# Weights' parts and lower rows at other byte offsets in a decoder layer's products

## The chip, the cores and the metric

The kernel runs on one core of a Trainium2 chip. It computes one inference step of a decoder layer in a single launch. The metric is the device time of that launch in microseconds; the time before is the median of 3 runs. A traced execution of the same kernel gives the profile, in microseconds unless marked ns.

## The reference

There are 288 tokens: 256 of a prompt and 8 groups of 4 sample tokens. The model's width is 2048. What is computed, cut to its core:

```python
h = rms_norm(x, norm1)
z = h @ w_in            # queries, keys, values, gates: 12 816 columns
q, k, v, (...) = split(z)
o_swa = sliding_window_attention(q, k, v, sink)
o_g = gated_linear_attention(...)         # per-head norm, swish gate
y = sigmoid(gs) * (o_swa @ p_swa) + sigmoid(gg) * (o_g @ p_gla)
x = x + y @ w_o
h2 = rms_norm(x, norm2)
x = x + square(relu(h2 @ w_up)) @ w_down  # 2048 -> 8192 -> 2048
y_out = rms_norm(x, final_norm)
```

The attention caches and the recurrent states are outputs too. All is float32.

## The kernel before

**Layout.** Activations stand with features on the 128 partitions and the 288 tokens along the free dimension: a tensor of 2048 features is 16 rows of 288 values on each partition. A matrix product has a 128x128 piece of the weights as the stationary operand and a row of 288 values as the moving one.

**Three products for one.** Each operand is split into an upper part (the value rounded to the format `fp32r`) and a lower part (what is left, in `fp32r` as well). Each piece of a product is then three products on TensorE: upper row by upper weight, lower row by upper weight, upper row by lower weight. The upper and lower rows are called `hh` and `hl` in the input projection, `o` (eight rows of upper and eight of lower parts in one tile) for `ps`, `gh` and `gl` for `pg`, `yh` and `yl` for `wo`, `h2h` and `h2l` for `up`, `uh` and `ul` for `dn`.

**The loop.** `gemm` (L222) makes 512 output columns of one product. It loads the weights in chunks of 256 rows by 512 columns (`raw`, six buffers, issued on SP's queue at L233). For each half of a chunk `wsplit` (L215) has ScalarE write the upper part `whi` (L218) and VectorE the lower part `wlo` (L156), five buffers each. A chunk is 24 products on TensorE (L251): two rows k by four slices m of 128 columns by the three of the split. In the first and the last chunk of a group the two rows alternate after every three products; in between all of one row come first. Four PSUM banks collect the results, and `evac` moves them out.

**Stages.** The order is the list `ORDER`: the input projection with the two attentions interleaved in small steps (`pump`), with `ps` in the middle; then `rg`, `pg` (four groups), `wo` (four groups), and four blocks b of `up{b}` (four groups) and `dn{b}` (four groups). A group has 8 chunks, in `ps` 4.

**Addresses.** Rows made by `rows` (L180) are 320 values apart, 1280 bytes, of which 288 are used, and start at multiples of 256 bytes; so do the buffers of `whi` and `wlo` (2048 bytes each). The rows of `o` are 288 values apart, 1152 bytes: every second one starts 128 bytes behind a multiple of 256. The weights `qx` of the attention's scores (L454) use two neighbouring buffers of 1152 bytes (tags `rs_m` and `rs_t`), the first at a multiple of 256, the second 128 bytes behind one.

**Other names in this text.** `ones` and `onesr` are the same 128x128 ones in float32 and `fp32r`. `maskp` is the mask of the prompt's scores, `masks` that of the samples' scores; the latter stands in the tile `ya`, in rows not yet needed. `at` is the gated attention's 128x384 matrix of products within a block: ScalarE copies it out of PSUM (L756, L757), GpSimd zeroes what lies ahead in time (L759), and TensorE uses it as the moving operand of `po` (L780, L781). `en` is a tile of that attention whose two buffers are read by the products that make `at`. `rso` is the tag of the two factors `rstd2` and `rstd3` of the last norms.

Of the kernel before, what the change touches and what calls it, by code (L numbers as in the profile page):

```python
# [12 lines left out]
F32 = mybir.dt.float32  # L13
F32R = mybir.dt.float32r
AF = mybir.ActivationFunctionType
ALU = mybir.AluOpType
# [3 lines left out]
P = 128  # L20
# [6 lines left out]
NT = TP + TS  # L27
# [31 lines left out]
def swa_rows():  # L59

    rows = []
    for p in range(2):
        for r in range(4):
# [8 lines left out]
         + ["qk2", "v2", "gg0", "gg1", "qk3", "v3", "gg2", "gg3"] + [f"rg{i}" for i in range(4)]  # L72
         + [f"pg{i}" for i in range(4)] + [f"wo{i}" for i in range(4)]
         + [x for b in range(4) for x in ([f"up{b}_{i}" for i in range(4)] + [f"dn{b}_{i}" for i in range(4)])])


def chunks_of(name):
    return 4 if name.startswith("ps") else 8
# [53 lines left out]
def step_kernel(ctx: ExitStack, tc: tile.TileContext, a: dict):  # L132
    nc = tc.nc
    V, S, G, T, SY = nc.vector, nc.scalar, nc.gpsimd, nc.tensor, nc.sync
    main = ctx.enter_context(tc.tile_pool(name="main", bufs=1))
# [4 lines left out]
    def f(ap):  # L140
        return ap.bitcast(F32)

    def bank(name):
        return psm.tile([P, 512], F32, name=name, tag="sm")

    def flat(ap):
        return ap.rearrange("p a b -> p (a b)")
# [7 lines left out]
    def sub(out, x, y, eng=V):  # L155
        eng.tensor_tensor(out, x, y, ALU.subtract)  # L156
# [1 line left out]

    ident = main.tile([P, P], F32, name="ident")
    norms = main.tile([P, 36], F32, name="norms")  # L160
    ones = main.tile([P, P], F32, name="ones")
    onesr = main.tile([P, P], F32R, name="onesr")
    epst = main.tile([P, 1], F32, name="epst")
    bm = main.tile([P, 32 + NB + 34], F32, name="bm")
# [4 lines left out]
    raw0 = main.tile([P, 1024], F32, name="raw", tag="raw", bufs=RAW)  # L169
    for s in range(2):  # L170
        S.dma_start(raw0[:, 512 * s:512 * s + 512], a["w"][0, :, 512 * s:512 * s + 512])
    V.memset(ones, 1.0)
    V.tensor_copy(onesr, ones)
    V.memset(epst, EPS)
    n2, fn, gn = norms[:, 0:16], norms[:, 16:32], norms[:, 32:36]

    def big(tag, name, dt=F32, n=KT):
        return main.tile([P, n, NT], dt, name=name, tag=tag)

    def rows(tag, name, n=KT):  # L180

        return main.tile([P, n, 320], F32R, name=name, tag=tag)[:, :, 0:NT]

    def exp_table():
        tc.keep_in_program_order(S.preload_act_table_set("natural_log_exp_and_others"))
# [16 lines left out]
    def pump(rates):  # L202
        for i, r in enumerate(rates):
            credit[i] += r
            while credit[i] >= 1.0:
                credit[i] -= 1.0
                if not step(queues[i]):
                    credit[i] = 0.0
# [3 lines left out]
            pass  # L212


    def wsplit(raw):  # L215
        hi = main.tile([P, 512], F32R, name="whi", tag="whi", bufs=5)
        lo = main.tile([P, 512], F32R, name="wlo", tag="wlo", bufs=5)
        S.copy(hi, raw)  # L218
        sub(lo, raw, f(hi))
        return hi, lo  # L220

    def gemm(name, xh, xl, evac, rate=(), first=None):  # L222
        nk = 2 * chunks_of(name)
        ps = [pmm.tile([P, 512], F32, name="mm", tag="mm") for _ in range(4)]
        for c in range(nk // 2):
            if FIRST[name] + c == 0:
                raw = raw0
            else:
                raw = main.tile([P, 1024], F32, name="raw", tag="raw", bufs=RAW)
                if first is not None:  # L230
                    first[0](c, raw)
                else:
                    SY.dma_start(raw, a["w"][FIRST[name] + c])  # L233
            parts = []
            for s in range(2):
                if first is not None:
                    first[1](2 * c + s)
                parts.append((2 * c + s, *wsplit(raw[:, 512 * s:512 * s + 512])))
            if first is not None:
                first[2](c)  # L240

            turns = c == nk // 2 - 1 or c == 0 and first is None
            order = [(i, m) for m in range(4) for i in range(2)] if turns else [(i, m) for i in range(2) for m in range(4)]
            order = [(i, m, j) for i, m in order for j in range(3)]
            if c == 0 and first is not None:

                order[:12] = [(0, m, j) for j in range(3) for m in range(4)]
            for i, m, j in order:
                k, hi, lo = parts[i]
                o, sl = ps[m][:, :NT], slice(m * P, m * P + P)  # L250
                T.matmul(o, lhsT=(lo if j == 2 else hi)[:, sl], rhs=xl(k) if j == 1 else xh(k),  # L251
                         start=k == 0 and j == 0, stop=k == nk - 1 and j == 2)
                if k == nk - 1 and j == 2:
                    evac(m, o)
            pump(rate)
# [39 lines left out]

    xa = big("SG", "x")
    hh, hl = rows("XH", "hh"), rows("XL", "hl")
    xn = []

# [97 lines left out]
    def swa(pool):  # L397
        rope = pool.tile([P, 2, NT], F32, name="rope")
        SY.dma_start(flat(rope), a["rope"])
        vt = pool.tile([P, 2, 2, P], F32, name="vt")  # L400
# [1 line left out]
        sinkb = pool.tile([P, 16], F32, name="sinkb")  # L402
        nsinkb = pool.tile([P, 16], F32, name="nsinkb")
        sinkr = pool.tile([P, 1], F32, name="sinkr")
        maskp = pool.tile([P, 384], F32, name="maskp")
        masks = ya[:, 8:12]
        SY.dma_start(sinkb, a["sinkb"])
        SY.dma_start(sinkr, a["sinkr"])
# [151 lines left out]
        po = bank("os")  # L560
        pov = po.rearrange("p (a b c) -> p a b c", a=4, b=2)
        sn = pool.tile([TS, 4, P], F32, name="stn", tag="sc", bufs=2)
        for pr in range(4):
# [8 lines left out]
            for p in range(2):  # L572
                for b in range(2):
                    T.matmul(pov[:, pr, p], lhsT=vc[p][:, 2 * pr + b], rhs=st[:, P * b + 64 * p:P * b + 64 * p + 64],  # L574
                             start=pr == 0 and p == 0 and b == 0, stop=False, skip_group_check=True)
# [32 lines left out]
    with tc.tile_pool(name="swa", bufs=1) as spool:  # L608
        RS = (1.05,)

        ya = big("YA", "ya")
# [7 lines left out]
    gpool = ctx.enter_context(tc.tile_pool(name="gla", bufs=1))  # L619
# [19 lines left out]
    def gla(h):  # L639
# [24 lines left out]
        vt = gpool.tile([P, 2, 512], F32, name="vtok", tag="vtok")  # L664
# [9 lines left out]
        for t in range(2):  # L674
            e = main.tile([P, 9, P], F32, name="e", tag=f"Za{2 + t}")
            en = gpool.tile([P, 2, P], F32, name="en", tag="en", bufs=2)
# [42 lines left out]
        pa = bank("pa")  # L719
# [32 lines left out]
            for work in tiled.pop():  # L752
                work()
        yield
        at = gpool.tile([P, 384], F32, name="at")
        S.copy(at, pa[:, :384])  # L756
        S.copy(at[0:64, 320:384], pa[64:P, 384:448])  # L757
        for sl, n in ((slice(0, 256), 256), (slice(256, 384), P)):
            G.affine_select(out=at[:, sl], in_=at[:, sl], pattern=[[1, n]], compare_op=ALU.is_ge, fill=0.0, base=0,  # L759
                            channel_multiplier=-1)  # L760
        yield
        parts = h < 3
        kdt = gpool.tile([P, 2, 256], F32R if parts else F32, name="kdt", tag="B")
# [12 lines left out]
        for jj in range(2):  # L776
            po = bank("po")
            for j in range(2):
                vsl = slice(P * (2 * jj + j), P * (2 * jj + j) + P)
                T.matmul(po[:, 256 * j:256 * j + 256], lhsT=vt[:, 0, vsl], rhs=at[:, 0:256], start=True, stop=False)  # L780
                T.matmul(po[:, 256 * j + P:256 * j + 256], lhsT=vt[:, 1, vsl], rhs=at[:, 256:384], start=False, stop=True)  # L781
            S.copy(o_g[:, 2 * jj:2 * jj + 2, 0:TP], po.rearrange("p (a b) -> p a b", a=2))
            if parts:
                S.copy(vh[:, jj], vt[:, jj])
                for c in (slice(0, 256), slice(256, 512)):
                    lo = main.tile([P, 256], F32R, name="vl", tag=("zr", "sr")[jj], bufs=2)
                    sub(lo, vt[:, jj, c], f(vh[:, jj, c]))
                    vl.append(lo)
            yield
# [120 lines left out]
    def start_head(h):  # L910
        queues[0].append(gla(h))
        queues[1].append(gla_sample(h))
# [5 lines left out]
    for j in range(4):  # L918
        sl = slice(4 * j, 4 * j + 4)
# [21 lines left out]
    for j in range(4):  # L941
        sl = slice(4 * j, 4 * j + 4)
# [3 lines left out]
    gh, gl = {}, {}  # L946
    for h in range(4):
        gh[h] = rows(f"Za{(0, 2, 3, 1)[h]}", f"gh{h}", 4)
        tt = main.tile([P, 4, NT], F32, name="tt", tag="tt")

        def rg_evac(m, ps):
            zr = main.tile([P, NT], F32, name="zr", tag="zr", bufs=2)
            sr = main.tile([P, NT], F32, name="sr", tag="sr", bufs=2)
            mul(zr, ps, rstd1)
            S.activation(sr, zr, AF.Sigmoid)
            mul(zr, zr, sr)
            mul(tt[:, m], og[h][:, m], zr)
            S.copy(gh[h][:, m], tt[:, m])
        if h == 2:
            late.append(True)  # L960
        gemm(f"rg{h}", H, L, rg_evac, rate=R3)
        if h == 1:
            drain(0)
        if h == 2:
            drain(1)
        gl[h] = rows(f"Zb{h}", f"gl{h}", 4)
        sub(gl[h], tt, f(gh[h]))
# [3 lines left out]
    yh, yl = rows("XH", "yh"), rows("XL", "yl")  # L971
# [15 lines left out]
    h2h = [rows(f"Za{j}", f"h2h{j}", 4) for j in range(4)]  # L987
    h2l = [rows(f"Zb{j}", f"h2l{j}", 4) for j in range(4)]
    acc2 = main.tile([P, NT], F32, name="acc2", tag="acc")
    rstd2 = main.tile([P, NT], F32, name="rstd2", tag="rso", bufs=2)  # L990

    def square_sum(acc, x, start):
        if start:
# [59 lines left out]


    acc3 = main.tile([P, NT], F32, name="acc3", tag="acc")
    rstd3 = main.tile([P, NT], F32, name="rstd3", tag="rso", bufs=2)
    last = []
    parts3 = []

# [70 lines left out]
    for n in (1, 1, 2, 2, 2, 2, 2, 2, 1, 1):  # L1130
        sl = slice(i, i + n)
# [57 lines left out]
def build(arrays):  # L1189
    nc = bacc.Bacc("TRN2", target_bir_lowering=False, num_devices=1)  # L1190
    aps = {}
    for n, v in arrays.items():
        aps[n] = nc.dram_tensor(f"in_{n}", v.shape, mybir.dt.from_np(v.dtype), kind="ExternalInput").ap()
    for n, s in OUTS.items():
        aps[n] = nc.dram_tensor(f"out_{n}", s, F32, kind="ExternalOutput").ap()
    with tile.TileContext(nc) as tc:
        step_kernel(tc, aps)
    return nc
# [21 lines left out]
```

## Time and profile before

| | us |
|---|---|
| time, median of 3 runs | 1754.13 |
| lowest and highest run | 1753.87, 1754.18 |
| the profiled execution | 1756.34 |
| its span | 1754.6 |
| TensorE busy in it | 1743.0 |
| VectorE busy | 1209.0 |
| ScalarE busy | 878.3 |

A profiled execution's span runs from its first to its last instruction. The lines by group give source line, engine, operation, output and inputs by tile name, shapes and count, then busy time, mean of one in ns, and the engine's idle time before them with what ended it. The weight load of a product has a row of its own (PEld) and overlaps the product before. Products overlap too: one lasts 0.29 us from its first to its last value, while the next starts much sooner, so the rate is read from starts or from counts in a window, not from the length of one. The DMA engines moved 214 GB/s on average; the weights come in ahead of their use:

```profile
raw<-in_w SPq DMA_DIRECT2D x518, 512.0 KB, 4.0
HBM read 348.58 MB, written 23.92 MB: 212 GB/s over the span
```

### The profile page before, as it was taken

Reading aid. Unit: us, or ns where it says so; the run is one execution under the profiler, and the core shown is the slowest. Engines: PE = TensorE matmul, PEld = TensorE weight load, DVE = VectorE, ACT = ScalarE, POOL = GpSimd, SP = SyncE. Lnnn points to the kernel's source line nnn. Section 1 sums busy time; section 2 is a strip of 40 time slices with the busy share of each in tenths; the row PEclk is TensorE's granted clock in tenths of the full one; section 3 lists DMA queues with packets and bytes.
Section 4 is the critical chain, followed back from the end, with each engine's and each line's share of the span. In section 5 each row is a group of like instructions: output and inputs, shape, how many; then the busy total and the mean of one; then the engine's idle time right before and its main releaser. Section 6 shows DMA issues by size and latency. Waiting matters only on the chain.

```text
span 1754.6 us, 34457 instructions
## 1 busy us (share of the span) xinstructions
PE 1743.0 (99%) x13463; PEld 1714.7 (98%) x13463; DVE 1209.0 (69%) x2270; ACT 878.3 (50%) x1650; POOL 63.4 (4%) x75
## 2 busy tenths in 40 slices
PE   9999999999999999999999999999999999999997
PEld 8999999999999999999999999999999999999997
DVE  8896574665836657666688677767777777777545
ACT  7555464444534645544445554455544554455543
POOL 0000001001001010000131000000000000000000
PEclk9999999999999999999999999999999999999998
DMA  8645446455464455444866777776777667765552
GB/s 296 213 140 181 135 162 228 158 192 207 158 234 167 159 217 180 165 165 154 326 213 210 263 253 260 276 263 240 249 256 286 237 233 287 269 247 201 191 176 95
DMA packets 102884, 374.74 MB, mean 214 GB/s; under 512 B 12481, under 2 KB 15041, under 8 KB 98625
## 3 DMA queue, kind: packets, MB, share of 16 engines
q1 hardware_dynamic: 102144, 371.49, 60.1%
q8 instruction: 105, 1.72, 0.4%
q10 hardware_dynamic: 576, 1.05, 0.2%
q14 instruction: 59, 0.48, 0.1%
HBM read 348.58 MB, written 23.92 MB: 212 GB/s over the span
## 4 chain that ended last, share of the span: by engine, by line
PE 99%; DVE 1%; issue 0%; ACT 0%; DVEq 0%
PE mm L251 94%; PE pos L870 1%; PE score L454 0%; PE po L780 0%; PE o L498 0%; PE pt L486 0%; PE warm L379 0%; DVE x L150 0%; PE po L781 0%; PE os L574 0%; PE pv L668 0%; PE pa L723 0%; PE pst L803 0%; PE ssq L260 0%; PE pst L801 0%; PE pst L804 0%
## 5 line engine op out<-in xcount | busy, mean ns | idle before, releaser
L156 DVE TENSOR_TENSOR wlo<-raw,whi 128x512 fp32r<-128x512 f32 x1040 | 714.4, 700 | 456.5 <-ACT whi L218 452.3
L218 ACT CAST whi<-raw 128x512 fp32r<-128x512 f32 x1040 | 629.9, 618 | 729.8 <-PE mm L251 673.4
L251 PE MATMUL mm<-hh,whi 128*128 128x288 f32 x1472 | 437.9, 298 | 0.0
L251 PE MATMUL mm<-hh,wlo 128*128 128x288 f32 x1472 | 432.5, 294 | 0.0
L251 PE MATMUL mm<-hl,whi 128*128 128x288 f32 x1472 | 432.4, 294 | 0.0
L251 PE MATMUL mm<-h2h,wlo 128*128 128x288 f32 x1024 | 301.2, 294 | 0.0
L251 PE MATMUL mm<-uh,wlo 128*128 128x288 f32 x1024 | 301.1, 294 | 0.0
L251 PE MATMUL mm<-uh,whi 128*128 128x288 f32 x1024 | 301.1, 294 | 0.0
L251 PE MATMUL mm<-ul,whi 128*128 128x288 f32 x1024 | 301.1, 294 | 0.0
L251 PE MATMUL mm<-h2h,whi 128*128 128x288 f32 x1024 | 301.0, 294 | 0.0
L251 PE MATMUL mm<-h2l,whi 128*128 128x288 f32 x1024 | 301.0, 294 | 0.0
L251 PEld LDWEIGHTS mm<-hh,whi 128*128 128x128 f32 x1472 | 276.7, 188 | 5.5 <-issue 3.0
L251 PEld LDWEIGHTS mm<-hl,whi 128*128 128x128 f32 x1472 | 276.7, 188 | 0.2
L251 PEld LDWEIGHTS mm<-hh,wlo 128*128 128x128 f32 x1472 | 276.0, 188 | 0.8 <-DVE wlo L156 0.5
L251 PEld LDWEIGHTS mm<-h2h,wlo 128*128 128x128 f32 x1024 | 192.1, 188 | 0.3 <-DVE wlo L156 0.3
L251 PEld LDWEIGHTS mm<-h2l,whi 128*128 128x128 f32 x1024 | 192.1, 188 | 0.0
L251 PEld LDWEIGHTS mm<-h2h,whi 128*128 128x128 f32 x1024 | 192.1, 188 | 0.0
L251 PEld LDWEIGHTS mm<-uh,whi 128*128 128x128 f32 x1024 | 192.1, 188 | 0.0
L251 PEld LDWEIGHTS mm<-ul,whi 128*128 128x128 f32 x1024 | 192.1, 188 | 0.0
L251 PEld LDWEIGHTS mm<-uh,wlo 128*128 128x128 f32 x1024 | 192.1, 188 | 0.0
L1028 DVE SCALAR_TENSOR_TENSOR acc_s<-vb,kdk,acc_s 128x512 f32<-128x512 f32 x192 | 144.5, 757 | 3.0 <-ACT acc_s L1026 2.7
L251 PE MATMUL mm<-yh,wlo 128*128 128x288 f32 x256 | 75.0, 294 | 0.4 <-DVE wlo L156 0.4
(282 smaller groups left out, 1814.3 us busy)
## 6 DMA issues: line engine op xcount, KB each, us to landing
raw<-in_w SPq DMA_DIRECT2D x518, 512.0 KB, 4.0
raw<-in_s SPq DMA_DIRECT2D x64, 512.0 KB, 4.4
vb<-vd SPq DMA_DIRECT2D x32, 1024.0 KB, 6.8
out_ssn<-raw SPq DMA_DIRECT2D x32, 512.0 KB, 4.8
x<-in_x SPq DMA_DIRECT2D x4, 576.0 KB, 5.7
x<-in_x SPq DMA_DIRECT2D x6, 288.0 KB, 7.6
out_y<-x SPq DMA_DIRECT2D x6, 288.0 KB, 2.7
out_sp<-so SPq DMA_DIRECT2D x6, 256.0 KB, 2.0
```

What stands on the lines that cost most here:

```text
L156: eng.tensor_tensor(out, x, y, ALU.subtract)
L218: S.copy(hi, raw)
L251: T.matmul(o, lhsT=(lo if j == 2 else hi)[:, sl], rhs=xl(k) if j == 1 else xh(k), start=k == 0 and j == 0, stop=k == nk - 1 and j == 2)
L870: T.matmul(pos[r:r + 32], lhsT=qm[:, t, 32 * b:32 * b + 32], rhs=st[i + g][:, 512 * t:512 * t + 512], start=b < 2, stop=b >= NB - 2)
L1028: paced(V.scalar_tensor_tensor(acc[t], v(n), k(n), acc[t], ALU.mult, ALU.add))
```

## The change

The buffers of `whi` and `wlo` grow from 512 to 576 values (2304 bytes, so each still begins at a multiple of 256), and `wsplit` uses 512 of them from an offset that depends on the stage: 64 bytes in up0, 192 in up1, 32 in up2, 256 in dn0, 96 in dn1, 16 in dn2, and 0 in up3, dn3 and all other stages. The rows of `yl` begin 64 bytes further in their 1280, those of `gl` 128. Ten buffers of 256 bytes more need room, and four edits make it: `ones` becomes a view of `onesr`, `maskp` moves into rows 12 and 13 of `ya`, `at` becomes two tiles in the buffers of `en`, and `rso` has one buffer. What is computed stays the same.

```diff
+OFFSET = {"up0": 16, "up1": 48, "up2": 8, "dn0": 64, "dn1": 24, "dn2": 4}
-    ones = main.tile([P, P], F32, name="ones")
+    ones = f(onesr)
     V.memset(ones, 1.0)
-    V.tensor_copy(onesr, ones)
     def rows(tag, name, n=KT):
-        return main.tile([P, n, 320], F32R, name=name, tag=tag)[:, :, 0:NT]
+        off = {"yl": 16, "gl": 32}.get(name[:2], 0)
+        return main.tile([P, n, 320], F32R, name=name, tag=tag)[:, :, off:off + NT]
-    def wsplit(raw):
-        hi = main.tile([P, 512], F32R, name="whi", tag="whi", bufs=5)
-        lo = main.tile([P, 512], F32R, name="wlo", tag="wlo", bufs=5)
+    def wsplit(raw, off):
+        hi = main.tile([P, 576], F32R, name="whi", tag="whi", bufs=5)[:, off:off + 512]
+        lo = main.tile([P, 576], F32R, name="wlo", tag="wlo", bufs=5)[:, off:off + 512]
-                parts.append((2 * c + s, *wsplit(raw[:, 512 * s:512 * s + 512])))
+                parts.append((2 * c + s, *wsplit(raw[:, 512 * s:512 * s + 512], OFFSET.get(name.split("_")[0], 0))))
-        maskp = pool.tile([P, 384], F32, name="maskp")
+        maskp = flat(ya[:, 12:14])[:, 0:384]
-        at = gpool.tile([P, 384], F32, name="at")
-        S.copy(at, pa[:, :384])
-        S.copy(at[0:64, 320:384], pa[64:P, 384:448])
-        for sl, n in ((slice(0, 256), 256), (slice(256, 384), P)):
-            G.affine_select(out=at[:, sl], in_=at[:, sl], pattern=[[1, n]], compare_op=ALU.is_ge, fill=0.0, base=0,
-                            channel_multiplier=-1)
+        at = [gpool.tile([P, n], F32, name="at", tag="en", bufs=2) for n in (256, P)]
+        for x, sl in zip(at, (slice(0, 256), slice(256, 384))):
+            S.copy(x, pa[:, sl])
+        S.copy(at[1][0:64, 64:P], pa[64:P, 384:448])
+        for x, n in zip(at, (256, P)):
+            G.affine_select(out=x, in_=x, pattern=[[1, n]], compare_op=ALU.is_ge, fill=0.0, base=0, channel_multiplier=-1)
-    rstd2 = main.tile([P, NT], F32, name="rstd2", tag="rso", bufs=2)
+    rstd2 = main.tile([P, NT], F32, name="rstd2", tag="rso")
-    rstd3 = main.tile([P, NT], F32, name="rstd3", tag="rso", bufs=2)
+    rstd3 = main.tile([P, NT], F32, name="rstd3", tag="rso")
```

On TensorE the order of products is the same before and after. It changes in two places on other engines. The first is ScalarE where the first head's `at` is copied, in the stage gs3; before:

```order
L218 CAST whi<-raw 128x512 x3
L756 COPY at<-pa 128x384
L757 COPY at<-pa 64x64
L218 CAST whi<-raw 128x512
L920 ACTIVATE ya<-ya 128x1152
L185 ACT_TABLE_LOAD
```

and after, where line numbers are up to five higher:

```order
L222 CAST whi<-raw 128x512 x3
L761 COPY at<-pa 128x256
L761 COPY at<-pa 128x128
L762 COPY at<-pa 64x64
L222 CAST whi<-raw 128x512
L924 ACTIVATE ya<-ya 128x1152
L189 ACT_TABLE_LOAD
```

One copy has become two, and the next cast of weights stands behind one instruction more. The second place is SP's queue where the attention's masks are loaded, early in the program; before:

```order
L410 DMA ya<-in_masks 128x1152
L233 DMA raw<-in_w 128x1024
L426 DMA out_vp<-swa_kv 128x128
L428 DMA out_vsn<-swa_kv 128x32
L426 DMA out_vp<-swa_kv 128x128
L233 DMA raw<-in_w 128x1024
L399 DMA rope<-in_rope 128x576
L407 DMA sinkb<-in_sinkb 128x16
L408 DMA sinkr<-in_sinkr 128x1
L409 DMA maskp<-in_maskp 128x384
L428 DMA out_vsn<-swa_kv 128x32
```

and after:

```order
L413 DMA ya<-in_maskp 128x384
L237 DMA raw<-in_w 128x1024
L414 DMA ya<-in_masks 128x1152
L430 DMA out_vp<-swa_kv 128x128
L432 DMA out_vsn<-swa_kv 128x32
L237 DMA raw<-in_w 128x1024
L403 DMA rope<-in_rope 128x576
L411 DMA sinkb<-in_sinkb 128x16
L412 DMA sinkr<-in_sinkr 128x1
L430 DMA out_vp<-swa_kv 128x128
L432 DMA out_vsn<-swa_kv 128x32
```

The strip `maskp` has moved to the front and `masks` behind the next chunk of weights; the loads of weights keep their order.

More of the change, by code (lines that the diff above doesn't have):

```diff
@@ L779, in gla @@
                 vsl = slice(P * (2 * jj + j), P * (2 * jj + j) + P)
-                T.matmul(po[:, 256 * j:256 * j + 256], lhsT=vt[:, 0, vsl], rhs=at[:, 0:256], start=True, stop=False)
-                T.matmul(po[:, 256 * j + P:256 * j + 256], lhsT=vt[:, 1, vsl], rhs=at[:, 256:384], start=False, stop=True)
+                T.matmul(po[:, 256 * j:256 * j + 256], lhsT=vt[:, 0, vsl], rhs=at[0], start=True, stop=False)
+                T.matmul(po[:, 256 * j + P:256 * j + 256], lhsT=vt[:, 1, vsl], rhs=at[1], start=False, stop=True)
             S.copy(o_g[:, 2 * jj:2 * jj + 2, 0:TP], po.rearrange("p (a b) -> p a b", a=2))
```

## The prediction

> **What bounds the kernel.** I read the page first, then the chain of waits in order of time, then a window over the long quiet part.
>
> ```profile
> span 1754.6 us, 34457 instructions
> PE 1743.0 (99%) x13463; PEld 1714.7 (98%) x13463; DVE 1209.0 (69%) x2270; ACT 878.3 (50%) x1650; POOL 63.4 (4%) x75
> ...
> PEclk9999999999999999999999999999999999999998
> ...
> PE 99%; DVE 1%; issue 0%; ACT 0%; DVEq 0%
> ...
> L156 DVE TENSOR_TENSOR wlo<-raw,whi 128x512 fp32r<-128x512 f32 x1040 | 714.4, 700 | 456.5 <-ACT whi L218 452.3
> L218 ACT CAST whi<-raw 128x512 fp32r<-128x512 f32 x1040 | 629.9, 618 | 729.8 <-PE mm L251 673.4
> ```
>
> TensorE is busy 99% of the span and carries 99% of the chain. The two engines that make the weights' parts wait for it: ScalarE (L218) stands 673 us waiting for TensorE to free a buffer, and VectorE (L156) waits for ScalarE. So what happens to the split costs nothing until it is slower than TensorE, and the time is the number of products by the distance from one start to the next.
>
> ```profile
> 686.85 222.84 PE mm L251 x1691
> ...
> 941.12 797.91 PE mm L251 x6060
> ...
> 1040.00:1640.00 600.00, 600.00 (x4559) 600.00 (x4559) 0.95 0.72 255
> ```
>
> The first two rows are from the chain, the third is a window of L251 alone. The last stretch of the chain is 797.91 us for 6060 products without a break: 131.67 ns each. The stretch before it gives 131.8 (222.84 over 1691), and the window agrees (600 us over 4557, since two of the 4559 only reach into it) and shows the granted clock, 0.95, and no idle time. So rows and weights at multiples of 256 bytes give one spacing, whatever the stage and its other work. A change of 1 ns in it over one block of the up or down products (4 groups by 8 chunks by 24, 768 products) is 0.77 us; 0.2% of the whole, 3.5 us, is about what a measurement of this kernel can tell from no change.
>
> **The shifted rows (gl by 128 bytes, yl by 64).** Every product of before reads weights at a multiple of 256 bytes. One stage of before reads rows elsewhere: the ps products read o, whose rows are 1152 bytes long, so that even rows begin at a multiple of 256 and odd ones 128 behind it.
>
> ```profile
> 334.77 0.43 PE L251 MATMUL mm<-o,whi 128*128 128x288 f32 x2
> ...
> 336.35 0.43 PE L251 MATMUL mm<-o,whi 128*128 128x288 f32 x2
> ...
> 337.95 0.43 PE L251 MATMUL mm<-o,whi 128*128 128x288 f32 x2
> ...
> 368.21 0.42 PE L251 MATMUL mm<-o,whi 128*128 128x288 f32 x2
> ...
> 374.61 0.43 PE L251 MATMUL mm<-o,whi 128*128 128x288 f32 x2
> ```
>
> These rows of the timeline are starts (first column) in two places of that stage. From 334.77 stand 12 products on an even row: 1.58 us, 131.7 ns each. From 336.35 stand 12 on the next, odd row: 1.60 us, 133.3 ns. From 368.21 to 374.61 the order changes the row after every third product, and 48 products take 6.40 us: 133.3 ns, for the even rows too. So a row that begins 128 bytes off costs 1.67 ns a product, and in a mixture its neighbours pay as well.
>
> In pg the order of a group of three is upper row, lower row, upper row; after the change the lower one begins 128 bytes off. If only that product pays, it is 256 by 1.67 ns, 0.43 us; if all three pay, as in the mixture, 768 by 1.67 ns, 1.28 us. I take 1.28, since the mixture is the nearer row. In wo the shift is 64 bytes, which no row shows. Its bounds are those of the neighbours at 0 and 128 bytes, 0 and 1.28 us; a gain has its price below, with the rivals. I take the middle, 0.64.
>
> [...]
>
> **The shifted weights (16 to 256 bytes in up and down).** The buffers are now 2304 bytes, nine times 256, so all ten still begin at multiples of 256, and the slice read begins the block's offset behind that. dn0 (256 bytes) and block 3 (none) stay where they were in this sense; up0, up1, up2, dn1 and dn2, 5 by 768 products, do not. Nearest to it are the scores of the attention: weights qx in one of two buffers, the first at a multiple of 256, the second 1152 bytes on, so 128 off.
>
> ```profile
> 70.35 1.07 PE L454 MATMUL score<-kx,qx 128*128 128x128 f32 x8
> ...
> 70.81 0.50 PE L454 MATMUL score<-kx,qx 128*128 128x128 f32 x3
> ...
> 71.26 0.29 PE L251 MATMUL mm<-hh,whi 128*128 128x288 f32 x1
> ```
>
> The first four of the eight use the buffer at 0, the other four that at 128, with the same rows: 70.35 to 70.81 is 0.46 us, 70.81 to 71.26 is 0.45 us. No cost of a weight's shift is seen, though these products are shorter (128 and 256 columns). For the up and down products I bound it above by the worst row for rows, 3840 by 1.67 ns or 6.4 us, and below by the whole spare time of a product, priced under the rivals; I take 0, the scores' value. Writing the parts at an offset costs ScalarE and VectorE at most what hides behind the 673 us of waiting quoted above; uncovered, 10 ns on each of the 1040 casts would be 10 us.
>
> [...]
>
> **The small edits.** They make room. The mask strip in ya moves one load ahead in SP's queue and lets the mask's load follow one weight chunk later; no weight load is added. The copy of at in two pieces adds one ScalarE instruction per head.
>
> ```profile
> 268.95 0.48 ACT L756 COPY at<-pa 128x384 f32<-128x384 f32 x1 [2.01 <-PE pa L723]
> ...
> 269.51 0.65 POOL L759 TENSOR_SCALAR_AFFINE_SELECT at<-at 128x256 f32<-128x256 f32 x2 [269.00 <-ACT at L756]
> ...
> L780 PEld LDWEIGHTS po<-at,vtok x32: 187/190/198, 284.2 to 646.6; 128*128 128x128 f32 x32
> ...
> 1.53 0.16 DVE L173 CAST onesr<-ones 128x128 fp32r<-128x128 f32 x1
> ...
> 1.67 4.02 PE L379 MATMUL warm<-warm 128*128 128x512 bf16 x9 [1.67 <-DVE warm L376]
> ```
>
> GpSimd is done with at by 270.16, and TensorE first loads for po at 284.2: 14 us cover the added copy, which is at most 0.48 us a head, 1.9 us in all if the cover were gone. GpSimd's added waits are for VectorE's and TensorE's use of en, over before pa could be copied. Behind the waiting select stands only its twin, and the square sums of a later step. The cast that goes (0.16 us) lies beside the warm-up products. The tiles of the gated attention's pool now begin 128 bytes off; the 32 products with at and 48 with kdt or kdl pay at most 80 by 1.67 ns, 0.1 us. The single rso buffer is asked for the second time after the last product, when the readers of the first are long through. I cost all of it at 0.
>
> **Sum.** 1.28 + 0.64 + 0 = 1.92 us. The profiled execution took 1756.34 us (span 1754.6 and 1.7 around it) and would take 1758.3; the median of the runs before is 1754.13, 2.2 under it, and the same sum on it gives **1756.0**. Its own range is 0.43 to 2.56 us more: 1754.5 to 1756.7.
>
> **Rivals.** *Nothing moves.* The odd rows of ps pay because upper and lower row are both off there; with an aligned row on each side the shifted one hides in the stall that every product has: 0 us, 1754.1. For it: one product in three is shifted, not all. Against it: in the mixture at 368.21 nothing was hidden. [...]
>
> *Slower: the distance of weights from rows decides.* In ps the odd rows also stood 128 bytes from the weights. If that distance is what costs, each of the five blocks pays up to 1.28 us, on top of pg and wo: 1754.13 + 6.4 + 1.92 = 1762.5, and 1763.1 with wo in full. It decides from the second block: two of them, 2.56 us, with the forecast's 1.92 make 4.5 us, over 3.5, where one makes 3.2. For it: the excess is per product, as a collision at each load of weights would be. Against it: the scores.
>
> *Faster: a distance that avoids a stall.* A product has spare time to lose.
>
> ```profile
> 293.78 0.39 PE L804 MATMUL pst<-vh,kdl 128*128 128x512 f32 x1
> ...
> 294.24 0.40 PE L803 MATMUL pst<-vl,kdt 128*128 128x256 f32 x2
> ```
>
> Two products of 512 columns start between these, 0.23 us each. Against 131.67 ns for 288 columns that is 0.44 ns a column, so 288 columns alone would need 126.4 ns and 5.3 ns are stall. A block that lost all of it gains 768 by 5.3 ns, 4.1 us; all five and wo give 24 us, 1730. One block without cost elsewhere gives 1750.0. Against it: the one other alignment that the trace shows, the odd rows of ps, is worse and not better.
>
> **How the numbers follow.** Forecast 0.42, nothing moves 0.20, distance costs 0.28 (0.02 of it under 3.5 us), a gain 0.10 (0.02 of it under 3.5 us). Faster by over 0.2% is 0.08, within 0.2% 0.42 + 0.20 + 0.02 + 0.02 = 0.66, slower 0.26. The range reaches over the slower rival and leaves out the gain and the end of that rival: 1753.2 to 1763.0, with some 0.12 outside.
>
> **What would show it.** Chain or windows after the change, products per time in each block: pg at 133.3 ns, wo between 131.7 and 133.3, all up and down blocks at 131.67, dn0 and block 3 in any case. Slower rival: up0, up1, up2, dn1, dn2 near 133.3 while block 3 stays. Faster: one of them nearer 126. The forecast is wrong if pg stays at 131.67, if a block with shifted weights leaves it, or if L251 shows idle time before loads of weights from whi or wlo.

## The result, and the profile after

| | before | after |
|---|---|---|
| median of 9 runs each, us | 1754.18 | 1758.53 |
| lowest and highest, us | 1753.87, 1754.78 | 1758.12, 1758.99 |
| the profiled execution, us | 1756.34 | 1758.99 |

The change costs 4.35 us, a ratio of 1.0025 with a 95% interval of 1.0014 to 1.0035: slower, by 0.25%, with the interval's lower end under 0.2%. The range held it, the likeliest case did not come, and the chance given to slower was 0.26.

From the page of the kernel after, the totals, the clock, the chain and the two groups that make the weights' parts:

```profile
span 1757.3 us, 34466 instructions
...
PE 1745.6 (99%) x13463; PEld 1718.3 (98%) x13463; DVE 1208.9 (69%) x2269; ACT 878.5 (50%) x1654; POOL 63.6 (4%) x75
...
PEclk9999999999999999999999999999999999999999
...
PE 99%; DVE 1%; issue 0%; ACT 0%; DVEq 0%
...
L160 DVE TENSOR_TENSOR wlo<-raw,whi 128x512 fp32r<-128x512 f32 x1040 | 713.7, 698 | 459.0 <-ACT whi L222 456.2
L222 ACT CAST whi<-raw 128x512 fp32r<-128x512 f32 x1040 | 630.1, 618 | 731.2 <-PE mm L255 679.6
```

The picture is the same: TensorE carries 99% of the chain, and the makers of the parts wait for it as long as before (679.6 us against 673.4). A cast takes 618 ns and a subtraction 698 (before 618 and 700), so writing at an offset shows no cost in these means. What changed stands in the chain of waits, whose last pieces are (start, length, products):

```profile
685.39 215.18 PE mm L255 x1631
...
910.89 28.68 PE mm L255 x214
939.84 801.88 PE mm L255 x6060
```

The last 6060 products took 797.91 us and now take 801.88, 132.32 ns each for 131.67: 3.97 us, most of the 4.35 between the medians. The spans differ by less, 2.7 us, because the profiled execution of before reached this stretch 1.28 us later; it was 2.2 us above its median, as the prediction noted.

The windows of the products' line show which stages paid. A row has the window, TensorE's busy time with the products that touch the window, the same of the weight loads, the granted clock, and the DMAs' share and rate. Two of the products only reach in. The first row lies in `pg`, the second in `wo`, the others in dn0, up1, dn1, up2, dn2 and up3; after:

```profile
755.00:825.00 70.00, 70.00 (x532) 70.00 (x531) 1.00 0.51 174
...
855.00:903.00 48.00, 48.00 (x368) 48.00 (x367) 1.00 0.67 242
...
1034.00:1132.00 98.00, 98.00 (x746) 98.00 (x745) 1.00 0.76 273
1135.00:1233.00 98.00, 98.00 (x747) 98.00 (x745) 1.00 0.68 243
1236.00:1335.00 99.00, 99.00 (x745) 99.00 (x744) 1.00 0.77 271
1339.00:1437.00 98.00, 98.00 (x738) 98.00 (x737) 1.00 0.67 242
1441.00:1539.00 98.00, 98.00 (x744) 98.00 (x744) 1.00 0.76 275
1542.00:1640.00 98.00, 98.00 (x746) 98.00 (x745) 1.00 0.66 232
```

The same view of before, in `pg`, `wo` and dn1:

```profile
756.00:826.00 70.00, 70.00 (x534) 70.00 (x533) 0.95 0.52 174
...
856.00:904.00 48.00, 48.00 (x367) 48.00 (x366) 0.95 0.67 240
...
1237.00:1335.00 98.00, 98.00 (x746) 98.00 (x745) 0.95 0.78 276
```

dn0, up1 and up3 have 744 to 745 products in 98 us as before; up2 has 736, 133.2 ns each, dn1 743 in 99 us, 133.2; `pg` lost two in 70 us and `wo` won one in 48. No window has idle time: the products stand further apart, and nothing waits. Taken from the first starts of the products, group by group, the spacings and what they make over 768 products against 131.67 ns are:

```
stage           pg      wo      up0     dn0     up1     dn1     up2     dn2     up3, dn3
weights at, B   0       0       64      256     192     96      32      16      0
ns              132.22  131.11  133.33  131.67  131.67  133.33  133.33  132.00  131.67
us              +0.42   -0.43   +1.28   0       0       +1.28   +1.28   +0.25   0
```

The sum is 4.08 us. So the time came from three of the blocks whose weights were shifted, with a little from a fourth. (`wo` settles at 131.11 only within its first group; from its first product to the first of up0 it took 0.24 us less than before, so 0.43 is what the steady spacing makes of 768 products.)

### The profile page after: what moved, and what is told of

The parts are those of the page before. It is cut to its first block, busy times and chain, and to the rows that moved or that the text cites. A ratio compares the mean times of both kernels' runs of the same rounds, so it can differ in the third digit from the quotient of the medians.

```text
span 1757.3 us, 34466 instructions
## 1 busy us (share of the span) xinstructions
PE 1745.6 (99%) x13463; PEld 1718.3 (98%) x13463; DVE 1208.9 (69%) x2269; ACT 878.5 (50%) x1654; POOL 63.6 (4%) x75
## 4 chain that ended last, share of the span: by engine, by line
PE 99%; DVE 1%; issue 0%; ACT 0%; DVEq 0%
PE mm L255 93%; PE pos L874 1%; PE score L458 0%; PE po L784 0%; PE o L502 0%; PE pt L490 0%; PE warm L383 0%; DVE x L154 0%; PE os L578 0%; PE po L785 0%; PE pv L672 0%; PE pa L727 0%; DVE wlo L160 0%; PE pst L807 0%; PE pst L808 0%; PE pst L805 0%
## 5 line engine op out<-in xcount | busy, mean ns | idle before, releaser
L222 ACT CAST whi<-raw 128x512 fp32r<-128x512 f32 x1040 | 630.1, 618 | 731.2 <-PE mm L255 679.6
L255 PE MATMUL mm<-gh,whi 128*128 128x288 f32 x256 | 75.6, 296 | 0.0
```

## The experiments

All kernels below are built from the kernel after, with its longer buffers and room edits. In most of them the offset table has one entry per group for the upper and one for the lower part of the weights, and a second table shifts rows; numbers in the code are values of 4 bytes, in the text bytes.

```diff
-    def wsplit(raw, off):
-        hi = main.tile([P, 576], F32R, name="whi", tag="whi", bufs=5)[:, off:off + 512]
-        lo = main.tile([P, 576], F32R, name="wlo", tag="wlo", bufs=5)[:, off:off + 512]
+    def wsplit(raw, oh, ol):
+        hi = main.tile([P, 576], F32R, name="whi", tag="whi", bufs=5)[:, oh:oh + 512]
+        lo = main.tile([P, 576], F32R, name="wlo", tag="wlo", bufs=5)[:, ol:ol + 512]
...
-        off = {"yl": 16, "gl": 32}.get(name[:2], 0)
+        off = ROWS.get(name if blk is None else f"{name}{blk}", 0)
```

**The room alone.** All offsets are 0; the buffers stay long and the four edits that make room stay.

```diff
-OFFSET = {"up0": 16, "up1": 48, "up2": 8, "dn0": 64, "dn1": 24, "dn2": 4}
+OFFSET = {}
+ROWS = {}
```

> Change kept, but every offset of weights and rows set to 0: only the longer buffers and the four edits that make room are left. Both theories (distance between weights and rows; address of the weights alone): the 4.35 us come from the offsets, so the time is that of before within 0.5 us, 1753.7 to 1754.7, every up, down, pg and wo group at 131.67 ns a product. Rival that the edits that make room cost: part of the 4.35 us stays, over 1755.5.

Measured: 1754.35 us (10 runs) against 1754.33, ratio 1.0001 (0.9991 to 1.0010). The last stretch of its chain, and the window of the products that the prediction showed of before:

```profile
939.25 797.91 PE mm L256 x6060
```

```profile
1040.00:1640.00 600.00, 600.00 (x4559) 600.00 (x4558) 1.00 0.71 255
```

Length and count are those of before to the last digit. So the change's cost comes from the offsets. Before showed a granted clock of 0.95 in this window and this kernel 1.00; the spacing is the same, 131.67 ns, so that figure says nothing of it.

**The weights alone.** The shifts of `yl` and `gl` go, the weights keep theirs.

```diff
-        off = {"yl": 16, "gl": 32}.get(name[:2], 0)
+        off = 0
```

> The change without the shift of yl and gl: weights' offsets alone. Distance theory, with the spacings of the maps (133.33 ns at 64, 32 and 96 bytes, 132.0 at 16, 131.67 at 192, 256 and 0): three blocks by 768 products by 1.67 ns and one by 0.33 are 3.84 + 0.25 = 4.1 us more than before, 1758.4; pg and wo back at 131.67. If the rows had carried a net part of the 4.35 us, it would lie nearer to before.

Measured: 1758.29 us (10 runs) against 1754.15, ratio 1.0023 (1.0014 to 1.0033). Its windows in `pg` and `wo`, and the last stretch of its chain:

```profile
755.00:825.00 70.00, 70.00 (x534) 70.00 (x533) 1.00 0.51 175
855.00:903.00 48.00, 48.00 (x367) 48.00 (x366) 1.00 0.67 242
```

```profile
939.01 801.88 PE mm L255 x6060
```

`pg` and `wo` are back at their counts of before, and the last stretch is that of after, 801.88 us. The weights' shifts alone cost 4.1 us; the rows' shifts move `pg` and `wo` in opposite directions and nearly cancel.

**The map of offsets.** Three theories were open: the distance of weights from rows decides, the weights' own address does, or the rows' does. In the first kernel the rows are at 0, each group of `up` has both parts at another multiple of 16 bytes, and `dn` has pairs.

```diff
+OFFSET = {f"up{b}_{i}": (4 * (4 * b + i),) * 2 for b in range(4) for i in range(4)}
+PAIRS = [(0, 4), (0, 8), (0, 16), (0, 32), (0, 48), (4, 0), (8, 0), (16, 0), (32, 0), (48, 0), (16, 48), (48, 16), (16, 32), (32, 16), (32, 32), (48, 32)]
+OFFSET |= {f"dn{b}_{i}": PAIRS[4 * b + i] for b in range(4) for i in range(4)}
```

> Rows of up and down at 0 (no row shifted in pg and wo either). The 16 groups of up have both weights' parts at 0, 16, 32, ... 240 bytes. The 16 groups of dn have upper and lower part apart: (0,16) (0,32) (0,64) (0,128) / (0,192) (16,0) (32,0) (64,0) / (128,0) (192,0) (64,192) (192,64) / (64,128) (128,64) (128,128) (192,128) bytes. From the changed kernel: 131.67 ns at 0, 132.0 at 16, 133.33 at 32, 64 and 96, 131.67 at 192. Both theories expect these again in up, with the same curve for rows that stay. Between 112 and 176 bytes nothing is known; the odd rows of ps let me expect 133.3 at 128. In dn a pair that differs should give other values than an equal one, as the shifted yl did (131.11).

In the second all rows of `up` begin at 64 and all of `dn` at 128, and both have the sixteen offsets.

```diff
+OFFSET = {f"{n}{b}_{i}": (4 * (4 * b + i),) * 2 for n in ("up", "dn") for b in range(4) for i in range(4)}
+ROWS = {f"h2{p}{j}": 16 for p in "hl" for j in range(4)} | {f"u{p}{b}": 32 for p in "hl" for b in range(4)}
```

> The same 16 steps of 16 bytes for both weights' parts in the groups of up and again in those of dn, but all rows of up (upper and lower) begin 64 bytes further and all rows of dn 128 bytes further. Theory distance: the curve of the kernel with rows at 0 comes back moved by 64 bytes in up (131.67 ns with the weights at 64, 132.0 at 80, 133.33 at 96, 128 and 160, 131.67 at 0) and by 128 in dn (131.67 at 128 and at 64, 133.33 at 160 to 224 and at 0). Theory address of the weights: the curve doesn't move: 131.67 at 0 and 192, 133.33 at 32 to 96, in up and dn alike. Theory address of the row alone: all groups of up give one value and all of dn another.

Times, one run each: 1759.65 and 1758.12 us. The spacing in ns, from the starts of the 144 products of the middle chunks of each group, by the distance D of weights from rows (weights less rows, modulo 256 bytes; for up0's first group without its three intervals over 200 ns, at a pause and at the norm's products):

```
D          0      16     32     48     64     80     96     112
rows 0     131.74 131.97 133.33 131.11 133.33 133.33 133.33 132.22
rows 64    131.67 131.98 133.33 131.11 133.33 131.11 133.33 132.22
rows 128   131.67 131.98 133.33 131.11 133.33 131.11 133.33 132.22

D          128    144    160    176    192    208    224    240
rows 0     133.33 131.11 131.67 132.64 131.67 132.22 133.33 131.67
rows 64    133.33 130.00 131.67 132.64 131.64 132.22 133.33 131.67
rows 128   133.33 131.11 131.67 132.64 131.67 132.22 133.33 131.67
```

Fourteen of the sixteen distances have one value wherever the rows stand. By the weights' own address the rows of the table wouldn't agree: weights at 64 bytes give 133.33 with rows at 0 and 131.67 with rows at 64 or 128. So in these two kernels it is the distance that decides, and the line for rows at 0 gives the stages of after: 133.33 at 64, 96 and 32, 131.97 at 16, 131.67 at 192 and 256. The odd rows of `ps` in the kernel before, 133.3 ns, are D = 128. Two distances, 80 and 144, have more than one value. The pairs in `dn` of the first kernel lie between 131.11 and 135.56 ns: the equal pair at 128 bytes has 133.33 as in `up`, and each of the ten with one part at 0 differs from the equal pair at its other offset.

**Parts apart.** First only the lower rows are shifted; then all rows are at 64, and one part of the weights is held at 208 while the other goes round.

```diff
+QUARTERS = [(x, y) for x in (0, 16, 32, 48) for y in (0, 16, 32, 48)]
+OFFSET = {f"up{b}_{i}": QUARTERS[4 * b + i] for b in range(4) for i in range(4)}
+LOW = (16, 32, 8, 4)
+OFFSET |= {f"dn{b}_{i}": ((i // 2) * LOW[b], (i % 2) * LOW[b]) for b in range(4) for i in range(4)}
+ROWS = {f"h2l{j}": 16 for j in range(4)} | {f"ul{b}": LOW[b] for b in range(4)}
```

> Only lower rows are shifted. up: lower rows at 64 bytes, weights' parts (upper, lower) at all 16 pairs of 0, 64, 128, 192. dn: lower rows at 64, 128, 32, 16 bytes in blocks 0 to 3, and in each block weights (0,0) (0,s) (s,0) (s,s) with s that shift. A group of three is upper row by upper weights, lower row by upper weights, upper row by lower weights, and the weights of the next product load while a product runs. If a row meets the weights loaded beside it, that is those of the next product, the lower row meets only the lower weights and the upper row only the upper: lower row and lower weights both at 64 (pair (0,64) in up and in dn0, (0,128) in dn1) is all at distance 0 and gives 131.67 ns. If a row meets its own weights, (0,64) has distances 0, -64 and +64 and gives another value. Known: (0,0) with 64 gives 131.11 and with 128 132.22, as wo and pg of the changed kernel. Some pair may lie below 131.1; the lowest seen spacing of single products is 126 ns.

```diff
+OFFSET = {f"up{b}_{i}": (52, 4 * (4 * b + i)) for b in range(4) for i in range(4)} | {f"dn{b}_{i}": (4 * (4 * b + i), 52) for b in range(4) for i in range(4)}
+ROWS = {f"h2{p}{j}": 16 for p in "hl" for j in range(4)} | {f"u{p}{b}": 16 for p in "hl" for b in range(4)}
```

> Rows of up and down all at 64 bytes. up: upper weights at 208 (distance 144), lower weights at 0 to 240 in steps of 16. dn: the same with upper and lower changed over. Distance theory: the two groups with both at 208 give 130.00 (or 131.11) ns, and each pair one value of the series 133.33 less 6.67 over a whole number, as in all maps so far. Two products of three read upper weights, so moving the upper part should change more than moving the lower. If one weight's distance decided alone, half of the curve would be flat.

Times 1758.16 and 1757.34 us, one run each. In the first, lower rows at 64 with upper and lower weights at (0, 0) gave 131.11 ns in `up` (behind the pause in its first group) and 131.85 in `dn`, (0, 64) 131.85 and 134.08: the same offsets, two values. Loads do lie beside the product ahead: in before's timeline one of `hh,whi` begins at 269.02, together with the product of `hh,wlo`, and its own product at 269.15. That a row meets only the next product's weights is not borne out, though: (0, 64), and (0, 128) with lower rows at 128, would then be 131.67, and the second gave 131.11. No pair lay below 131.11. In the second, both curves move, the upper fixed from 130.00 to 135.56, the lower fixed from 130.00 to 133.33. Neither part's distance decides alone. The expectation that moving the upper part, which two products of three read, would change more did not come: the wider spread, up to 135.56, is that of the moved lower part. Which load meets which product stays open.

**A distance that saves time.** D = 48 had 131.11 ns; it was put into all groups. The second kernel has D = 144 in the same way (rows at 64, weights at 208; `ps` as in the first).

```diff
+OFFSET = {name: (12, 12) for name in ORDER}
+ROWS = {}
```

> Both weights' parts 48 bytes behind a multiple of 256 in every stage, rows at 0, no lower row shifted. Distance theory: 131.11 ns where distance is 48 (three of three places of the maps), so 12096 products outside ps by 0.56 ns are 6.7 us less, and ps (distances 48 and 176, 131.1 and 132.6 against 131.7 and 133.3) 0.3 less: 1747.3. Rival, that a value holds only in the group and order where it was seen: the groups differ among themselves and the time stays over 1751.

```diff
+OFFSET = {name: (12, 12) if name.startswith("ps") else (52, 52) for name in ORDER}
+ROWS = {n: 16 for n in ["hh", "hl", "yh", "yl"] + [f"{g}{p}{i}" for g in ("g", "h2") for p in "hl" for i in range(4)] + [f"u{p}{b}" for p in "hl" for b in range(4)]}
```

> All rows but those of o begin 64 bytes further, and both weights' parts 208 bytes behind a multiple of 256: distance 144 (ps as in f48). The maps gave 130.00 ns there once (rows at 64) and 131.11 twice (rows at 0 and 128). If distance and the rows' own place set the spacing together, 130.00 throughout: 12096 by 1.67 ns, 1734. If what stands before the group decides which of the two it is, groups at 130.00 and at 131.11 stand side by side and the time lies between 1734 and 1747. If distance alone, one value: 1734 or 1747.

Measured: 1747.99 us (5 runs, ratio 0.9965, 0.9952 to 0.9978) and 1747.89 (6 runs, 0.9966, 0.9953 to 0.9978). Both beat the kernels before and after, and the first comes near the 1747.3 expected. The last stretch of the first:

```profile
936.12 794.56 PE mm L256 x6060
```

That is 131.11 ns, and against the kernel with the room alone, which reached this stretch at 939.25, 3.1 us were won ahead of it as well. The hope for 130.00 at D = 144 failed: 131.11 again, at offsets that had given 130.00 in one group.

**One pair, two spacings.** The second kernel with the parts apart had 130.00 with rows at 64 and weights at (208, 144). That pair was put into all groups, and in a second kernel the same distances with rows at 0.

```diff
-OFFSET = {name: (12, 12) if name.startswith("ps") else (52, 52) for name in ORDER}
+OFFSET = {name: (12, 12) if name.startswith("ps") else (52, 36) for name in ORDER}
```

> All rows 64 bytes off; upper parts of the weights at 208, lower parts at 144 bytes in all groups (ps as in f48), the pair that gave 130.00 ns in up2_1 of s4_apart. Theory that the addresses alone set the spacing: 130.00 ns in all groups, 12960 products by 1.67 ns less than 131.67, 21.6 us less, about 1733. Rival, that what ran before a group decides as well, as two groups at the same addresses of s4_apart had 130.00 and 131.11: 131.11 or more in many groups, 1747 or above.

```diff
+OFFSET = {name: (12, 12) if name.startswith("ps") else (36, 20) for name in ORDER}
+ROWS = {}
```

> Rows at 0, upper parts at 144 and lower parts at 80 bytes in all groups: the same two distances from the rows as in f130a, all addresses 64 bytes lower. Theory that the distance alone decides: the same spacing in each group and the same time as f130a to 0.1%, whatever that is. Rival, that the addresses themselves or the past matter as well: groups that differ from those of f130a by over 0.5 ns and times that differ by over 0.2%.

> The kernel f130b once more, in another series. If one kernel has two spacings, taken anew in each execution where TensorE comes out of a pause, its times fall near 1750 and near 1770 again, none between, and the profiled execution has up and down groups of 130.00 or of 133.33 ns and nothing else once the attention is over. If the two times were of that series alone: one time for all runs, within 0.2%.

Measured: the first 1771.65 us (4 runs, ratio 1.0099, 1.0082 to 1.0116), not the 1733 of the theory (which counted 12960 products; outside `ps` there are 12096). Its groups have 133.33 ns in `up` and `dn`. The second has two times (so its ratios, 1.0023 with 0.9985 to 1.0060 and 1.0068 with 1.0035 to 1.0101, are means over a mixture): in its two series 8 of 20 executions took 1748.9 to 1751.2 us and 12 took 1770.1 to 1771.5, none between. The two profiled executions fell on either side, and the slower one has the spacings of the first kernel in `up` and `dn`; four slow executions of the first, beside 12 of 20 of the second, don't set the two apart. Windows of the products' line in the faster one, ahead of the norm's products in up0, behind them, and over most of the rest:

```profile
936.00:943.00 7.00, 7.00 (x55) 7.00 (x54) 1.00 0.21 75
947.00:961.00 14.00, 14.00 (x110) 14.00 (x109) 1.00 0.84 281
1040.00:1640.00 600.00, 600.00 (x4617) 600.00 (x4617) 1.00 0.72 257
```

and in the slower one:

```profile
936.00:943.00 7.00, 7.00 (x55) 7.00 (x54) 1.00 0.24 77
947.00:961.00 14.00, 14.00 (x107) 14.00 (x106) 1.00 0.79 266
1040.00:1640.00 600.00, 600.00 (x4503) 600.00 (x4502) 1.00 0.70 252
```

One program, one set of addresses: 4615 products in 600 us against 4501, 130.0 ns against 133.3. Both ran at 133.33 ns in up0 up to 943 us. What lies between is in the timeline of the faster one (start, length):

```profile
944.29 0.40 PE L256 MATMUL mm<-h2h,wlo 128*128 128x288 f32 x1
944.53 0.29 PE L256 MATMUL mm<-h2h,whi 128*128 128x288 f32 x1
...
945.57 0.30 PE L256 MATMUL mm<-h2h,wlo 128*128 128x288 f32 x1
945.70 0.29 PE L275 MATMUL ssq<-ss_h,onesr 128*128 128x288 f32 x1
945.84 0.30 PE L276 MATMUL ssq<-ss_l,onesr 128*128 128x288 f32 x1
945.97 0.29 PE L256 MATMUL mm<-h2h,whi 128*128 128x288 f32 x1
```

There is a short pause at 944.29, where two starts lie 0.24 us apart. Right behind it, from 944.53 to 945.57, eight products take 1.04 us, 130.0 ns each, and behind the two products of the norm this rhythm lasts to the last product of the line, some 790 us on. In the slower execution the same pause leads back into the old one. A pause isn't needed for such a change: in both executions, and in the first kernel, the products went from 133.33 to 130.00 ns early in the seventh chunk of `wo`'s first group, with no two starts over 140 ns apart, and back to 133.33 behind a pause of 0.9 us in its last group. So one distance can have more than one steady rhythm, and it can change on the way, at a pause or without one; what picks the next one isn't shown.

**The map backwards.** As the second map, with the offsets in reversed order.

```diff
-OFFSET = {f"{n}{b}_{i}": (4 * (4 * b + i),) * 2 for n in ("up", "dn") for b in range(4) for i in range(4)}
+OFFSET = {f"{n}{b}_{i}": (60 - 4 * (4 * b + i),) * 2 for n in ("up", "dn") for b in range(4) for i in range(4)}
```

> As s2_rows, with the sixteen offsets in reversed order, from 240 bytes down to 0, so that each group follows another neighbour. Theory that the addresses alone set a group's spacing: each offset has its value of s2_rows again, rows at 64: 131.6, 132.2, 133.3, 131.7, 131.7, 132.0, 133.3, 131.1, 133.3, 131.1, 133.3, 132.2, 133.3, 130.0, 131.7, 132.6 for 0 to 240 bytes. Rival, that the state which a group inherits decides among several: the same set of values, but some offsets change theirs, 208 bytes (130.00 there) first of all; total within 1756 to 1760 in both cases.

Measured: 1758.56 us, one run. Of 32 groups 29 have the value of the second map again, within 0.1 ns. Three changed: D = 192 with rows at 64 and at 128, from 131.6 and 131.7 to 132.22, and D = 144 with rows at 64, from 130.00 to 131.11. The last one is seen by counts. In the second map's order and in the reversed one:

```profile
1565.50:1588.50 23.00, 23.00 (x179) 23.00 (x178) 1.00 0.78 262
```

```profile
981.50:1004.50 23.00, 23.00 (x177) 23.00 (x176) 1.00 0.73 264
```

Both theories hold in part. Most distances have one rhythm in these runs; three, 80, 144 and 192, have two. That the neighbour decides there isn't shown: each order ran once, and D = 80 came behind a group at D = 64 with 133.33 ns in both maps and yet gave 133.33 in one and 131.11 in the other.

## Why the prediction was right in part and wrong in its likeliest case

- **What bounds the kernel: right.** All the difference in time is the number of products by the change of their spacing, and 1 ns over a block is 0.77 us. The stages' sum, 4.08 us, meets the measured 4.35 within its interval.
- **The range, not the sum, held the time.** The sum's 1.92 us came from `pg` and `wo`, which nearly cancelled, and nothing was in it for the weights, which cost 4.1. The range reached far enough because it was drawn over the slower rival. By the prediction's own sign, a block with shifted weights that leaves 131.67 ns, the forecast was wrong.
- **The shifted weights, costed at 0: this step failed.** It took the scores' value, 0.46 us for four products at 0 against 0.45 at 128 bytes. The weights alone cost 4.1 us. The row could not have told: the cost sought was 1.67 ns a product, 0.007 us over four, less than the 0.01 us to which the row is given. A row that cannot resolve the effect is no evidence of zero. The upper bound, 1.67 ns a product, was what three blocks paid in full. Whether the scores' shorter products have rhythms of their own wasn't tried.
- **That the distance of weights from rows makes no difference, as the 0 implies: refuted by the maps.** With products of one length, 288 columns, and a granted clock of 1.00 in the windows taken of both maps, the distance alone moves the spacing with rows at 0 between 131.11 ns (D = 48) and 133.33 (D = 32). All offsets are multiples of 16 bytes, those at 131.11 as well as those at 133.33.
- **The slower rival: right in what it named, too simple in its size.** Distance decides, by the two maps, at fourteen of the sixteen steps. It charged all five blocks 1.28 us; three paid it, dn2 (16 bytes) a fifth and up1 (192) nothing, since the cost is no step from aligned to unaligned. That two blocks would be over 0.2% leaned on the 1.92 us of `pg` and `wo`; it took three and the part of a fourth.
- **`gl`, 1.28 us: mis-sized.** Measured 0.42, the lower bound, though not because one product in three pays: the starts repeat in a cycle of twelve, 129 to 136 ns apart, with a mean of 132.67 ns behind the upper row by upper weight, 132.92 behind the lower row and 131.08 behind the upper row by lower weight.
- **`yl`, 0.64 us between 0 and 1.28: wrong sign.** It gained, 0.43 us by the steady spacing. A gain was priced only under the rivals, so the term's bounds stopped at 0.
- **The small edits, 0: right,** by the kernel with the room alone.
- **The faster rival** was right that some distances beat the aligned one, and named no distance. It priced 5.3 ns a product as the most to win, an estimate that its own row doesn't give: two products of 512 columns in the 0.46 us from 293.78 to 294.24 are 0.449 ns a column, and 288 columns by that 129.4 ns, 2.3 under the 131.67, not 126.4. The lowest steady spacing of any run, 130.00, is 1.67 under the aligned one. A distance of 48 bytes in all groups gives a ratio of 0.9965.

What stays open is the cause beneath: whether and which reads of a product and of a load of weights collide, which of the neighbouring products they belong to, and what picks the rhythm. No run separates these.

## What to carry to other kernels

Where one engine streams without a pause and one spacing holds for hundreds of microseconds, try the byte distance between its two operands as a parameter, in steps of 16 bytes over 256, many values in one kernel, one group each: a cheap map, of which one column is worth 0.35% here (one kernel, products of 288 columns with new weights for each). Prefer a distance that gave one value wherever it was tried; a better one that has two can fall to the worse in the next execution, as one kernel did here (1748.9 to 1751.2 us in 8 executions, 1770.1 to 1771.5 in 12). And before a row is used as evidence that something costs nothing, compare its last digit with the cost sought.

## What was not expected of the hardware

- Most steady spacings lie on one ladder: 132.22, 131.67, 131.11, 130.00 ns are 133.33 less 6.67/n, for n = 6, 4, 3, 2; dn2's 132.00 is n = 5. In the five kernels with maps 129 of 155 groups of `up` and `dn` (all but the first) lie within 0.05 ns of 133.33 or one of these; others, such as 132.64 at D = 176, do not. The single starts repeat in short cycles: before, at 131.67, they stand 135, 131, 131, 130 ns apart; at D = 16, 129, 135, 130, 130, 136; in the faster execution at 130.00, 128, 128, 133, 129, 130, 132. So a cycle as a whole comes out shorter, by 6.67 ns for every n products, and none of these intervals is by itself 6.67 ns under 133.33; in after's up1, at 131.67 too, they stand 133, 132, 126 or 127, 135 ns apart, and there one in four is. The highest steady spacing seen, 135.56, lies 6.67/3 above 133.33. Why the unit has this size isn't known.
- A rhythm can outlive the group, the stage and the block: that at 130.00 ns ran from 946 us to the line's end over 6000 products, through every change of buffers and rows, and the same kernel ran 20 us longer in other executions.
